# Layer 1 of a two-layer decoder as one list of small steps in TensorE's order

## The chip, the cores and the metric

The kernel runs on one core of a Trainium2 chip. The metric is the device time of one execution in microseconds, as the median of three runs.

## The reference

The input x has 256 tokens of 1024 features. Layer 0 is stick-breaking attention and a squared-ReLU MLP; layer 1 is native sparse attention (NSA) and the same kind of MLP; a final norm ends it. The change touches layer 1's attention and the keys and values that it shares:

```python
kv = (hn @ w_kv).reshape(b, s, 3, 2, NSA_KV_GROUPS, HEAD_DIM)   # hn = rms_norm(h, kv_norm)
hid = jax.nn.gelu(jnp.einsum('bncgf,cfe->bncge', blk, cmp_w1))   # blk: windows of 32 tokens of kv[:, :, 0]
cmp = jnp.einsum('bncge,ced->bncgd', hid, cmp_w2)                # compressed keys and values
...
q = proj[..., :NSA_HEADS * DH]; gates = sigmoid(proj[..., NSA_HEADS * DH:] + gate_b)
q_rot = partial_rope(q)
p_cmp = softmax(q . k_cmp);  o_cmp = p_cmp . v_cmp               # masked
p_sel = softmax(q_rot . k_sel); p_w = softmax(q_rot . k_w)       # causal; selected blocks and window
o = gates[0] * o_cmp + gates[1] * o_sel + gates[2] * o_win
h = h + o @ w_o
```

There are 16 heads of 64 in 4 key groups. With 256 tokens all 4 blocks are selected and the window reaches all tokens, so both of these branches are dense causal attention.

## The kernel before

Every large product is computed in three matmuls: a float32 weight is split into a rounded part wh (a CAST on ACT, L96) and the rest wl (a subtract on DVE, L97), the activations likewise, and `mm3` (L146) issues the three products at L147, L148 and L149. Weights come as a stream of 1 MB loads. `feed` appends a load to the stream when the program is set up, and the stream is loaded and split in that order. `fetch` issues a load on SP into one of three raw buffers, when the second half of an earlier one has been split. `W(i)` forces load i to be split, in two halves; `step()` splits one half more if fewer than three loads lie ahead of the present one. The split tiles wh and wl are rings of three.

PSUM has eight banks in two rings of four: `bank` gives one of the first ("a"), `bank2` of the second ("z"). An engine that writes a bank waits until the readers of its last contents are done. A scheduler orders the instructions of ACT, DVE and POOL by their dependencies; PE keeps the program's order where `strict[0]` is set (L142).

Layer 1's attention is the function `nsa`. Its pieces, with the short names that this text gives them (a digit is the index of a load's first and second half, of a head pair or of a group):

- kv (`kv_proj`): a key/value projection, 8 blocks of `mm3` per half; ACT scales it out of PSUM (L534 and after).
- gt, `gather`, gp: transposes for the compressed windows, their assembly on DVE, ACT and POOL, and the gates.
- rt: a table for the rotation. kt (`keys_tr`): transposed keys. `keys_rope`: rotation of the keys on POOL.
- cw (`cw_proj`): the hidden layer of the compression, accumulated in one bank ph.
- q00, q01, ..., q31 (`q_proj`): half 0 or 1 of the query projection of group 0 to 3. After half 1 ACT copies the bank out (qu, L680), and the rotation follows: a shuffle on DVE (L683), a multiply on POOL (L684), a multiply and an add on DVE (L685, L686: qr).
- gelu (L697 to L707, ACT and DVE), ch (`cmp_kv`: transposes of the hidden layer, bank pht), ck (`cmp_kv2`: compressed keys kcb by DVE at L727, values vcb at L734, banks pkc and pvc).
- cp (`cmp_probs`): scores against the compressed keys (bank psc) and their softmax; ct (`cmp_tr`): its transposes (bank pct), copied by ACT to pcT.
- S0 to S7 (`scores`): eight score matmuls of a pair of heads into four banks z; eight reductions on DVE (L799: nm), eight exponentials on ACT (L801); then a reciprocal and a product with the gates on DVE (L803, L805: rs), and four multiplies on POOL (L810), which scale the probabilities pe. The scaling is called M0 to M7 here.
- T0 to T7 (`turn`): twelve transposes of pe into three banks ptp, copied to pT by ACT, DVE (the middle one, L825) and ACT.
- V0 to V7 (`values`): probabilities times values in a bank po; ACT and DVE take oT out of it (L230, L231).
- o000 and so on (`o_proj`: half of the rows, half of the columns, block): the output projection with oT, into four accumulators acc. Then the residual adds, and xn, the transposes for the MLP.

The order is written out by hand. PE does, after the first half of the second kv:

```
rt gt0 kv11 gt1 gp kv20 cw00 kv21 cw01 kt0 q00 kt1 q01 cw10 q10 cw11 S0 q11 S1 q20 q21 ch T0 S2 ck
q30 cp0 T1 S3 q31 ct0 V0 T2 S4 o000 V1 T3 cp1 S5 o001 V2 T4 ct1 S6 o002 V3 T5 S7 o003 V4 T6
o010 o011 V5 o012 T7 o013 V6 V7 o100 o101 o102 o103 (residual) o110 o111 xn o112 o113
```

Of the kernel before, what the change touches and what calls it, by code (L numbers as in the profile page):

```python
# [39 lines left out]
def hybrid_kernel(ctx, tc, x, xcols, eye, gcols, gfin, wqk, wv, wo0, wkv, wq, wg, rot, wo1, w1, w2, cw1, cw2, cpos, gate_b, consts, out):  # L40
# [85 lines left out]
    i_kv = [[feed(wkv[n, i], 2048) for i in range(2)] for n in range(2)]  # L126
    i_kv.append([feed(wkv[2, 0], 2048)])
    i_c = [[feed(cw1[0, 0], 2048)]]
    i_kv[2].append(feed(wkv[2, 1], 2048))
    i_c[0].append(feed(cw1[0, 1], 2048))  # L130
    i_q = [feed(wq[0], 2048)]
    i_c.append([feed(cw1[1, 0], 2048)])
    i_q.append(feed(wq[1], 2048))
    i_c[1].append(feed(cw1[1, 1], 2048))
    i_q += [feed(wq[g], 2048) for g in range(2, NG)]
    i_o1 = [[feed(wo1[n, i], 2048) for n in range(2)] for i in range(2)]
# [351 lines left out]
    def nsa(xk, pt0, ap):  # L488
# [145 lines left out]
        kv_proj(0, 0)  # L634
        kv_proj(0, 1)
        strict[0] = True
        xq = xt_tiles("q")
        for half in range(2):
            xt_evac(pts[half], half, 2, xq)
        kv_proj(1, 0)  # L640

        pr = bank2("pr")
        for t in range(T):
            mm(pr[:, t * P:(t + 1) * P], rstd[t].to_broadcast([P, P]), ident, t == 0, True)
        for a in range(2):
            nc.vector.scalar_tensor_tensor(cs[:, a, :], pr[:, 0:T * P], -1.0, cs[:, a, :], op0=OP.mult, op1=OP.mult)
        gather_tr(0)
        kv_proj(1, 1)
        gather_tr(1)
        gather(0)  # L650
        gate_proj()
        gather(1)
        keys_rope(0)
        ph = bank2("ph")
        kv_proj(2, 0)
        cw_proj(0, 0)
        kv_proj(2, 1)
        keys_rope(1)
        cw_proj(0, 1)
        kT = big([P, NG, 2, T * P], F32, "kT")  # L660
        keys_tr(0)
# [27 lines left out]
        q_proj(0, 0)
        keys_tr(1)  # L690
        qu = big([P, NG, 2, T * P], F32, "qu")
        qr = big([P, NG, 2, T * P], F32, "qr")
        q_proj(0, 1)
        cw_proj(1, 0)
        q_proj(1, 0)
        cw_proj(1, 1)
        hx = sp.tile([M, 512], F32, name="hx", tag="y")  # L697
        nc.scalar.copy(hx, ph[DH:DH + M, :])
        nc.vector.tensor_add(hx, ph[0:M, :], hx)
        hu = sp.tile([M, 512], F32, name="hu", tag="y")  # L700
        nc.scalar.activation(hu, hx, AF.Square, scale=0.044715 ** 0.5)
        nc.vector.scalar_tensor_tensor(hu, hu, 1.0, hx, op0=OP.add, op1=OP.mult)
        nc.vector.tensor_scalar(hu, hu, -25.0, None, op0=OP.max)
        nc.scalar.activation(hu, hu, AF.Exp, scale=-GELU_C)
        nc.scalar.activation(hu, hu, AF.Ln, bias=1.0)
        nc.scalar.activation(hu, hu, AF.Exp, scale=-1.0)
        nc.vector.tensor_mul(hu, hu, hx)  # L707

        def cmp_kv():
# [330 lines left out]
```

## Time and profile before

| | us |
|---|---|
| median of three runs | 639.63 (639.62 to 640.43) |
| the profiled execution's own time | 641.18 |
| its span | 639.4 |
| PE busy | 622.3 (97%) |
| DVE busy | 430.2 (67%) |
| ACT busy | 355.2 (56%) |
| POOL busy | 59.7 (9%) |

The profile is of one execution; times in its rows count from the start of the span. Layer 1's attention with its keys and values lies between 300 and 454 us. A matmul's busy time overlaps the next one's, so the length of a step is best read from its first start to the next step's first start. The granted clock is a share of full speed.

### The profile page before, as it was taken

The page shows a single profiled execution, that of the slowest core. Times are in us where ns is not written, and L with a number is a line of the kernel's source. Part 1 is how long each engine was busy: PE and PEld are TensorE (multiplying, and loading weights), DVE is VectorE, ACT ScalarE, POOL GpSimd, SP SyncE. Part 2 cuts the span into 40 slices and gives each one's busy share as a digit, 9 for nine tenths or more (in the row PEclk, how much of TensorE's full clock was granted, in tenths as well). Part 3 has the DMA queues.
Part 4 walks back from the last instruction along what each step waited for, and adds up shares of the span by engine and source line. Part 5 has one row for each costly group of instructions (what it writes and reads, how often), then busy time and mean ns, then how long its engine had stood idle before and what let it go on. Part 6 is the DMA issues. An engine that isn't in the chain of part 4 may idle for free.

```text
span 639.4 us, 9091 instructions
## 1 busy us (share of the span) xinstructions
PE 622.3 (97%) x3561; PEld 521.9 (82%) x3561; DVE 430.2 (67%) x672; ACT 355.2 (56%) x604; POOL 59.7 (9%) x78
## 2 busy tenths in 40 slices
PE   9999999999999999999999988999999999999995
PEld 6798987888888888888889776667888888888884
DVE  5677887676665656657896996662776566656554
ACT  5766666564444444443947875772564444454433
POOL 0100000000000000001151266350000000000000
PEclk9999999999999999999999998899999999999998
DMA  8953333545555554544456521203346455655501
GB/s 271 411 203 133 132 132 132 191 144 202 189 198 197 198 198 173 207 157 153 166 206 249 210 102 67 100 1 133 131 169 207 161 199 186 202 194 197 198 0 67
DMA packets 18331, 108.12 MB, mean 169 GB/s; under 512 B 2416, under 2 KB 3312, under 8 KB 6384
## 3 DMA queue, kind: packets, MB, share of 16 engines
q1 hardware_dynamic: 16992, 105.84, 46.1%
q10 hardware_dynamic: 1296, 1.70, 0.8%
q8 instruction: 28, 0.46, 0.3%
q14 instruction: 15, 0.12, 0.1%
HBM read 106.48 MB, written 1.05 MB: 168 GB/s over the span
## 4 chain that ended last, share of the span: by engine, by line
PE 83%; DVE 8%; ACT 3%; issue 2%; DMA 2%; POOL 1%; SPq 0%; POOLq 0%; ACTq 0%; DVEq 0%
PE pu L152 27%; PE acc L147 11%; PE acc L149 11%; PE acc L148 11%; PE po L152 3%; DVE wl L97 3%; PE z L152 2%; PE pk L147 2%; PE pk L149 2%; PE pk L148 2%; PE qk L147 1%; PE ptp L155 1%; PE qk L148 1%; PE qk L149 1%; ACT wh L96 1%
## 5 line engine op out<-in xcount | busy, mean ns | idle before, releaser
L97 DVE TENSOR_TENSOR wl<-raw,wh 128x1024 fp32r<-128x1024 f32 (+1 forms) x200 | 238.4, 1227 | 119.5 <-ACT wh L96 119.1
L96 ACT CAST wh<-raw 128x1024 fp32r<-128x1024 f32 (+1 forms) x200 | 197.6, 1033 | 100.0 <-PE acc L149 45.8
L152 PE MATMUL pu<-xn,wh 128*128 128x512 f32 x512 | 130.1, 392 | 0.6 <-DVE xn L222 0.6
L152 PEld LDWEIGHTS pu<-xn,wh 128*128 128x128 f32 x512 | 93.8, 188 | 19.6 <-DVE xn L222 1.8
L147 PE MATMUL acc<-wh,hh 128*128 128x512 f32 x256 | 100.2, 391 | 0.0
L148 PE MATMUL acc<-wl,hh 128*128 128x512 f32 x256 | 100.1, 391 | 0.0
L149 PE MATMUL acc<-wh,hl 128*128 128x512 f32 x256 | 99.6, 390 | 0.0
L152 PEld LDWEIGHTS pu<-xn,wl 128*128 128x128 f32 x512 | 70.9, 190 | 5.0
L152 PE MATMUL pu<-xn,wl 128*128 128x256 f32 x512 | 73.9, 282 | 0.0
L149 PEld LDWEIGHTS acc<-wh,hl 128*128 128x128 f32 x256 | 48.1, 188 | 10.7 <-DVE hl L311 0.4
L147 PEld LDWEIGHTS acc<-wh,hh 128*128 128x128 f32 x256 | 48.2, 188 | 9.7 <-ACT hh L310 0.6
L310 ACT CAST hh<-ms 128x512 fp32r<-128x512 f32 x32 | 19.8, 620 | 64.9 <-DVE ms L306 64.9
L148 PEld LDWEIGHTS acc<-wl,hh 128*128 128x128 f32 x256 | 48.2, 188 | 8.8
L304 ACT COPY mr<-pu 128x256 f32<-128x256 f32 x64 | 23.6, 369 | 29.2 <-PE pu L152 29.2
L147 PE MATMUL qk<-xa,wh 128*128 128x256 f32 x128 | 37.0, 289 | 0.0
L148 PE MATMUL qk<-xa,wh 128*128 128x256 f32 x128 | 36.2, 283 | 0.0
L149 PE MATMUL qk<-xa,wl 128*128 128x256 f32 x128 | 36.2, 283 | 0.0
L311 DVE TENSOR_TENSOR hl<-ms,hh 128x512 fp32r<-128x512 f32 x32 | 22.1, 691 | 19.9 <-ACT hh L310 19.9
L801 ACT ACTIVATE pe<-pe,nm 128x256 f32<-128x256 f32 (+1 forms) x64 | 28.3, 443 | 11.1 <-DVE nm L799 11.1
L810 POOL TENSOR_TENSOR pe<-pe,rs 128x512 f32<-128x512 f32 (+1 forms) x32 | 31.7, 1019 | 27.6 <-ACT oT L230 11.8
L305 DVE TENSOR_TENSOR mu<-pu,mr 128x256 f32<-128x256 f32 x64 | 26.7, 417 | 5.8 <-ACT mr L304 5.8
L149 PE MATMUL acc<-wh,oT 128*128 128x512 f32 x64 | 25.5, 398 | 2.3 <-DVE oT L231 2.3
(177 smaller groups left out, 881.9 us busy)
## 6 DMA issues: line engine op xcount, KB each, us to landing
raw<-in_w SPq DMA_DIRECT2D x64, 1024.0 KB, 4.8
raw<-in_wo SPq DMA_DIRECT2D x8, 1024.0 KB, 4.8
raw<-in_wqk SPq DMA_DIRECT2D x7, 1024.0 KB, 4.9
raw<-in_wkv SPq DMA_DIRECT2D x6, 1024.0 KB, 4.8
raw<-in_cw SPq DMA_DIRECT2D x4, 1024.0 KB, 5.2
raw<-in_wq SPq DMA_DIRECT2D x4, 1024.0 KB, 4.8
raw<-in_wv SPq DMA_DIRECT2D x8, 256.0 KB, 4.1
raw<-in_wv SPq DMA_DIRECT2D x4, 512.0 KB, 8.0
```

What stands on the lines that cost most here:

```text
L96: nc.scalar.copy(h[:, r], raws[j][:, r])
L97: nc.vector.tensor_sub(lo[:, r], raws[j][:, r], f32(h[:, r]))
L147: pe(nc.tensor.matmul(o, a[0], b[0], start=first, stop=False, skip_group_check=True))
L148: pe(nc.tensor.matmul(o, a[0], b[1], start=False, stop=False, skip_group_check=True))
L149: pe(nc.tensor.matmul(o, a[1], b[0], start=False, stop=last, skip_group_check=True))
L152: pe(nc.tensor.matmul(o, a, b, start=first, stop=last, skip_group_check=True))
L304: nc.scalar.copy(r[:, q], pu[f][:, 256:512])
L305: nc.vector.tensor_add(u[:, q], pu[f][:, 0:256], r[:, q])
L310: nc.scalar.copy(hh, sv)
L311: nc.vector.tensor_sub(hl, sv, f32(hh))
L801: nc.scalar.activation(e, e, AF.Exp, scale=-1.0, bias=nm[:, hd, t, b:b + 1], accum_out=rs[:, hd, t, b:b + 1])
L810: nc.gpsimd.tensor_tensor(sv, sv, rs[:, hd, t, :][:, :, None].to_broadcast([P, 2, n]), op=OP.mult)
```

## The change

A table `NSA` at the head of the file lists 104 steps of layer 1's attention, and a loop calls a function for each. The functions are those of before, cut smaller: the rotation (`q_rot`, "qr") is taken out of `q_proj`, the scaling (`weights`, "M") out of `scores`, and the gelu, the residual adds and xn are steps of their own. A turn, a score or a value step names the ring of each of its banks by a letter. The loads are fed in the order in which the list names their first use: kv20, kv21, c00, q0, c01 where it was kv20, c00, kv21, c01, q0. Six steps "w" call `step()` once more. The bank ph is of ring "a" now. PE keeps the list's order through the whole stage, where it was free to move the last part before.

```diff
+NSA = (
...
+    ('cw', 1, 1), ('q', 1, 1), ('S', 0, 'zzaz'), ('M', 0), ('ge',), ('qr', 1), ('S', 1), ('M', 1), ('q', 2, 0),
+    ('q', 2, 1), ('ch',), ('w',), ('T', 0, 'zaa'), ('S', 2, 'azaz'), ('ck',), ('q', 3, 0), ('T', 1), ('qr', 2),
...
+)
...
+    for f, *a in NSA:
+        if f == "kv":
+            i_kv[a[0]][a[1]] = feed(wkv[a[0], a[1]], 2048)
+        elif f == "cw":
+            i_c[a[0]][a[1]] = feed(cw1[a[0], a[1]], 2048)
+        elif f == "q" and a[1] == 0:
+            i_q[a[0]] = feed(wq[a[0]], 2048)
...
+        def q_rot(g, eng="p"):
...
+            nc.vector.stream_shuffle(qx, qu[:, g], swap)
+            (nc.gpsimd if eng == "p" else nc.vector).tensor_tensor(
+                qr[:, g], qu[:, g], cs[:, 0:1, :].to_broadcast([P, 2, T * P]), op=OP.mult)
...
-        def scores(p):
+        pools = {"a": bank, "z": bank2}
+
+        def scores(p, bks="zzzz"):
             g, j = divmod(p, 2)
-            z1 = [bank2(f"z1{hd}").rearrange("p (b k) -> p b k", b=2) for hd in range(2)]
+            z1 = [pools[bks[hd]](f"z1{hd}").rearrange("p (b k) -> p b k", b=2) for hd in range(2)]
...
+            live["s", p] = rs, pes
+
+        def weights(p):
+
+            rs, pes = live.pop(("s", p))
             nc.vector.reciprocal(rs, rs)
...
+        strict[0] = True
+        do = {"kv": kv_proj, "xq": tokens_q, "rt": rot_tables, "gt": gather_tr, "ga": gather, "gp": gate_proj, "kr": keys_rope,
+              "cw": cw_proj, "kt": keys_tr, "q": q_proj, "qr": q_rot, "ge": gelu, "ch": cmp_hid, "ck": cmp_kv, "S": scores,
+              "M": weights, "T": turn, "V": values, "cp": cmp_probs, "ct": cmp_tr, "o": o_proj, "r": residual, "xn": tokens_n,
+              "w": step}
+        for f, *a in NSA:
+            do[f](*a)
         strict[0] = False
```

Every engine has as many instructions as before. PE's order is now:

```
kv11 gt1 gp gt0 kv20 kv21 cw00 q00 cw01 rt kt0 q01 cw10 kt1 q10 cw11 q11 S0 S1 q20 q21 ch T0 S2 ck
q30 T1 cp0 S3 q31 ct0 V0 S4 V1 T2 cp1 T3 o000 S5 V2 ct1 T4 o001 S6 V3 V4 S7 T5 o002 o003 T6
o010 o011 V5 T7 o012 o013 o100 V6 V7 o101 o102 o103 (residual) o110 xn o111 o112 o113
```

Three places of the engines' order in detail. First PE at S0 and S1, before; ph is the end of cw11, z10 to z01 are the four banks of a pair's scores, pq is the half q11:

```order
L152 MATMUL ph_2967<-wh_3207,blk_2954 128x256
L152 MATMUL ph_2967<-wl_3208,blk_2954 64x256
L152 MATMUL z10_3283<-kT_3092,qr_3147 128x512
L152 MATMUL z11_3284<-kT_3092,qr_3147 128x512
L152 MATMUL z00_3285<-kT_3092,qr_3147 128x256
L152 MATMUL z01_3286<-kT_3092,qr_3147 128x256
L147 MATMUL pq_3206<-xq_2784,wh_3182 128x256
...
L149 MATMUL pq_3206<-xq_2784,wl_3183 128x256
L152 MATMUL z10_3351<-kT_3092,qr_3147 128x512
L152 MATMUL z11_3352<-kT_3092,qr_3147 128x512
L152 MATMUL z00_3353<-kT_3092,qr_3147 128x256
L152 MATMUL z01_3354<-kT_3092,qr_3147 128x256
```
And now:

```order
L166 MATMUL ph_3034<-wh_3187,blk_3094 128x256
L166 MATMUL ph_3034<-wl_3188,blk_3094 64x256
L161 MATMUL pq_3223<-xq_2678,wh_3149 128x256
...
L163 MATMUL pq_3223<-xq_2678,wl_3150 128x256
L166 MATMUL z10_3305<-kT_3136,qr_2677 128x512
L166 MATMUL z11_3306<-kT_3136,qr_2677 128x512
L166 MATMUL z00_3307<-kT_3136,qr_2677 128x256
L166 MATMUL z01_3308<-kT_3136,qr_2677 128x256
L166 MATMUL z10_3355<-kT_3136,qr_2677 128x512
L166 MATMUL z11_3356<-kT_3136,qr_2677 128x512
L166 MATMUL z00_3357<-kT_3136,qr_2677 128x256
L166 MATMUL z01_3358<-kT_3136,qr_2677 128x256
```
The half q11 stood between the two pairs of scores and now stands ahead of both; z00 of S0 is of the other ring.

Then PE at cp0 and T1, before; pq is the end of q30, psc is cp0, ptp are the three banks of T1, z10 is S3:

```order
L149 MATMUL pq_3528<-xq_2784,wl_3318 128x256
L152 MATMUL psc_3557<-kcb_3274,qu_3146 128x30 x8
L152 LDWEIGHTS cbf_76
L152 MATMUL psc_3557<-cmb_78,cbf_76 128x120
L152 LDWEIGHTS cbf_76
L152 MATMUL psc_3557<-cmb_78,cbf_76 128x120
L155 MATMUL ptp_3580<-ident_70,pe_3361 128x128 x4
L155 MATMUL ptp_3586<-ident_70,pe_3361 128x128 x2
L155 MATMUL ptp_3586<-ident_70,pe_3362 128x128 x2
L155 MATMUL ptp_3592<-ident_70,pe_3362 128x128 x4
L152 MATMUL z10_3598<-kT_3092,qr_3147 128x512
```
And now:

```order
L163 MATMUL pq_3521<-xq_2678,wl_3265 128x256
L169 MATMUL ptp_3551<-ident_70,pe_3365 128x128 x4
L169 MATMUL ptp_3557<-ident_70,pe_3365 128x128 x2
L169 MATMUL ptp_3557<-ident_70,pe_3366 128x128 x2
L169 MATMUL ptp_3563<-ident_70,pe_3366 128x128 x4
L166 MATMUL psc_3578<-kcb_2679,qu_2676 128x30 x8
L166 LDWEIGHTS cbf_76
L166 MATMUL psc_3578<-cmb_78,cbf_76 128x120
L166 LDWEIGHTS cbf_76
L166 MATMUL psc_3578<-cmb_78,cbf_76 128x120
L166 MATMUL z10_3606<-kT_3136,qr_2677 128x512
```
T1 and cp0 have changed places.

Then DVE behind the scaling factors of S3 (rs of L805), before; qx and qr are the rotation of q3, wl a half of a weight, oT of L231 what PE needs for o000, pT of L825 the middle of T2:

```order
L805 TENSOR_TENSOR rs_3607<-rs_3607,gates_2675 128x8
L683 STREAM_SHUFFLE qx_3661<-qu_3146 128x512
L685 TENSOR_TENSOR qx_3661<-qx_3661,cs_2664 128x512
L97 TENSOR_TENSOR wl_3918<-raw_3388,wh_3917 128x1024
L686 TENSOR_TENSOR qr_3147<-qr_3147,qx_3661 128x512
L231 TENSOR_TENSOR oT_3672<-po1_3673,oT_3672 128x256
L825 COPY pT_3686<-ptp_3693 128x512
L799 ISA pe_3715,nm_3713<-z10_3705,nmask_3280 128x256
```
And now, where pe and z10 are S4, the first oT is V0's and the second V1's:

```order
L822 TENSOR_TENSOR rs_3615<-rs_3615,gates_2675 128x8
L682 STREAM_SHUFFLE qx_3713<-qu_2676 128x512
L685 TENSOR_TENSOR qx_3713<-qx_3713,cs_2664 128x512
L112 TENSOR_TENSOR wl_3792<-raw_3278,wh_3791 128x1024
L811 ISA pe_3695,nm_3693<-z10_3685,nmask_2685 128x256
L811 ISA nm_3693 128x1
L245 TENSOR_TENSOR oT_3671<-po1_3672,oT_3671 128x256
L811 ISA pe_3695,nm_3693<-z10_3685,nmask_2685 128x256
...
L811 ISA pe_3696,nm_3693<-z01_3688,nmask_2685 128x128
...
L686 TENSOR_TENSOR qr_2677<-qr_2677,qx_3713 128x512
L112 TENSOR_TENSOR wl_3792<-raw_3278,wh_3791 128x1024
L245 TENSOR_TENSOR oT_3671<-po1_3718,oT_3671 128x256
```
The subtract for V0's oT stood behind the add of qr and now stands ahead of it, among the reductions of S4, which came after T2 before.

## Rows read from the trace of the kernel before

**Rows 1.** The page's first part: busy time, share of the span and instructions of each engine.
```profile
PE 622.3 (97%) x3561; PEld 521.9 (82%) x3561; DVE 430.2 (67%) x672; ACT 355.2 (56%) x604; POOL 59.7 (9%) x78
```

**Rows 2.** PE's waits, 250 to 460 us: instruction, what it waited for, us in total, times, longest.
```profile
PE acc L149 <- DVE oT L231: 2.3, 1, 2.3
PE ptp L155 <- ACT qu L680: 1.7, 1, 1.7
PE psc L152 <- DVE kcb L727: 1.2, 1, 1.2
PE acc L147 <- ACT oT L230: 1.0, 1, 1.0
PE z L152 <- DVE nm L799: 0.5, 1, 0.5
PE z L152 <- DVE qr L686: 0.5, 1, 0.5
```

**Rows 3.** Windows of 20 us: busy us of each engine, granted clock, DMA share, GB/s.
```profile
350.00:370.00 20.00, 19.01 (x145) 16.70 (x144) 18.33 (x44) 16.82 (x38) 5.70 (x5) 1.00 0.62 229
370.00:390.00 20.00, 17.06 (x126) 14.14 (x125) 17.93 (x59) 12.61 (x41) 12.45 (x12) 0.91 0.30 105
390.00:410.00 20.00, 17.73 (x123) 12.28 (x122) 13.43 (x48) 12.68 (x42) 9.01 (x9) 0.91 0.19 68
```

**Rows 4.** Timeline of PE, 380 to 389: start, us, instruction, idle before and releaser.
```profile
380.55 0.28 PE L149 MATMUL pq<-xq,wl 128*128 128x256 f32 x1
381.99 2.13 PE L152 MATMUL psc<-kcb,qu 128*128 128x30 f32 x16 [1.16 <-DVE kcb L727]
...
384.12 2.77 PE L155 MATMUL ptp<-ident,pe 128*128 128x128 f32 x12
```

**Rows 5.** Timeline of PE, 356 to 366: S0, the half q11, S1.
```profile
357.51 1.53 PE L152 MATMUL z<-kT,qr 64*128 64x512 f32 x6 [0.46 <-DVE qr L686]
359.57 0.67 PE L152 MATMUL z<-kT,qr 64*128 64x256 f32 x2 [0.53 <-DVE nm L799]
360.16 0.39 PE L147 MATMUL pq<-xq,wh 128*128 128x256 f32 x1
...
363.22 1.56 PE L152 MATMUL z<-kT,qr 64*128 64x512 f32 x8
```

**Rows 6.** Timeline of PE, 396 to 426: V1, T3, the second output block, V4.
```profile
401.24 2.83 PE L152 MATMUL po<-pT,vs 128*64 128x256 f32 x16
...
404.60 1.53 PE L155 MATMUL ptp<-ident,pe 128*128 128x128 f32 x12
...
409.58 0.50 PE L147 MATMUL acc<-wh,oT 128*128 128x512 f32 x1
...
424.73 1.52 PE L152 MATMUL po<-pT,vs 128*64 128x256 f32 x16
```

**Rows 7.** Timeline of POOL, 360 to 440: the scalings M0, M3, M4, M7.
```profile
367.44 4.08 POOL L810 TENSOR_TENSOR pe<-pe,rs 128x512 f32<-128x512 f32 x4
...
392.92 4.61 POOL L810 TENSOR_TENSOR pe<-pe,rs 128x512 f32<-128x512 f32 x4 [4.92 <-ACT qu L680]
...
405.08 3.18 POOL L810 TENSOR_TENSOR pe<-pe,rs 128x512 f32<-128x512 f32 x4 [6.32 <-ACT oT L230]
...
427.68 5.23 POOL L810 TENSOR_TENSOR pe<-pe,rs 128x512 f32<-128x512 f32 x4 [3.56 <-DVE rs L805]
```

**Rows 8.** The instructions of tile rs, 355 to 430: min/median/max ns of one.
```profile
L805 DVE TENSOR_TENSOR rs<-rs,gates x8: 154/173/1323, 366.0 to 427.3; 128x8 f32<-128x8 f32 x8
```

**Rows 9.** Timeline of DVE, 390 to 402: rotation of q3, then oT0.
```profile
398.79 0.69 DVE L686 TENSOR_TENSOR qr<-qr,qx 128x512 f32<-128x512 f32 x1 [2.30 <-POOL qr L684]
399.39 0.42 DVE L231 TENSOR_TENSOR oT<-po,oT 128x256 fp32r<-128x256 f32 x1
```

**Rows 10.** The page's DMA issues: count, KB each, us to landing.
```profile
raw<-in_cw SPq DMA_DIRECT2D x4, 1024.0 KB, 5.2
```

**Rows 11.** Timeline of PE, 452 to 456: the first matmul of the last MLP.
```profile
454.53 0.39 PE L152 MATMUL pu<-xn,wh 128*128 128x512 f32 x1
```

More of the change, by code (lines that the diff above doesn't have):

```diff
@@ L124, in hybrid_kernel @@
     i_m = [feed_mlp(0)]
[L126 to L136, printed above, removed]
+    i_kv, i_c, i_q, i_o1 = [{} for _ in range(3)], [{}, {}], {}, [{}, {}]
+    for f, *a in NSA:
[5 more added lines that the diff above has]
+            i_q[a[0]] = feed(wq[a[0]], 2048)
+        elif f == "o" and a[1] not in i_o1[a[0]]:
+            i_o1[a[0]][a[1]] = feed(wo1[a[1], a[0]], 2048)
     i_m.append(feed_mlp(1))
@@ L553, in nsa @@
         blk = [None, None]
+        ph = None
         def gather_tr(c):
@@ L586, in gather @@
             blk[c] = [b[:, j] for b in bs for j in range(n)]
+        kT = None
         def keys_rope(br):
@@ L599, in cw_proj @@
         def cw_proj(c, i):
+            nonlocal ph
+            if c == 0 and i == 0:
+                ph = bank("ph")
             w = W(i_c[c][i])
@@ L633, in nsa @@
         live = {}
[L634 to L661, printed above, removed]
+        qu = big([P, NG, 2, T * P], F32, "qu")
+        qr = big([P, NG, 2, T * P], F32, "qr")
         def q_proj(g, half, hooks={}):
@@ L689, in nsa @@
[L689 to L709, printed above, removed]
+        def q_rot(g, eng="p"):
+            qx = ap.tile([P, 2, T * P], F32, name="qx", bufs=2)
+            nc.vector.stream_shuffle(qx, qu[:, g], swap)
+            (nc.gpsimd if eng == "p" else nc.vector).tensor_tensor(
+                qr[:, g], qu[:, g], cs[:, 0:1, :].to_broadcast([P, 2, T * P]), op=OP.mult)
+            nc.vector.tensor_tensor(qx, qx, cs[:, 1:2, :].to_broadcast([P, 2, T * P]), op=OP.mult)
+            nc.vector.tensor_add(qr[:, g], qr[:, g], qx)
@@ new lines, in nsa, with tokens_q, rot_tables @@
+        swap = [*range(8, 16), *range(8), *range(16, 32)]
+        xq = xt_tiles("q")
+        def tokens_q(half):
+            xt_evac(pts[half], half, 2, xq)
+        def rot_tables():
+            pr = bank2("pr")
+            for t in range(T):
+                mm(pr[:, t * P:(t + 1) * P], rstd[t].to_broadcast([P, P]), ident, t == 0, True)
+            for a in range(2):
+                nc.vector.scalar_tensor_tensor(cs[:, a, :], pr[:, 0:T * P], -1.0, cs[:, a, :], op0=OP.mult, op1=OP.mult)
@@ new lines, in gelu @@
+        def gelu():
+            hx = sp.tile([M, 512], F32, name="hx", tag="y")
+            nc.scalar.copy(hx, ph[DH:DH + M, :])
+            nc.vector.tensor_add(hx, ph[0:M, :], hx)
+            hu = sp.tile([M, 512], F32, name="hu", tag="y")
+            nc.scalar.activation(hu, hx, AF.Square, scale=0.044715 ** 0.5)
+            nc.vector.scalar_tensor_tensor(hu, hu, 1.0, hx, op0=OP.add, op1=OP.mult)
+            nc.vector.tensor_scalar(hu, hu, -25.0, None, op0=OP.max)
+            nc.scalar.activation(hu, hu, AF.Exp, scale=-GELU_C)
+            nc.scalar.activation(hu, hu, AF.Ln, bias=1.0)
+            nc.scalar.activation(hu, hu, AF.Exp, scale=-1.0)
+            nc.vector.tensor_mul(hu, hu, hx)
+            live["h"] = hu
@@ L811, in scores, with turn @@
             live["e", p] = pes
-        def turn(p, bks=(bank, bank, bank)):
+        def turn(p, bks="aaa"):
             pes = live.pop(("e", p))
@@ L817, in turn @@
             for i in range(3):
-                pt = bks[i]("ptp")
+                pt = pools[bks[i]]("ptp")
                 for m in range(4):
@@ L828, in turn, with values @@
             live["t", p] = pT
-        def values(p, bk=bank):
+        oT = None
+        def values(p, bk="a"):
+            nonlocal oT
             g = p // 2
-            po = bk("po1")
+            if p == 0:
+                oT = pair([NP, T * P], "oT")
+                oT = oT[:, 0], oT[:, 1]
+            po = pools[bk]("po1")
             pT = live.pop(("t", p))
```

77 lines of the change are left out of this document (20 added, 57 removed), and 10 rows, old and new, of the table NSA.

## Prediction

> **What bounds the kernel now.** I read the page's first part, then TensorE's waits, then the windows, then the timelines of PE, DVE and POOL in the stretch that the change reorders. The page [rows 1] shows PE busy for 97% of the span, so the kernel is one long PE queue, and a reordering without new work can only win what PE now loses. The waits of PE between 250 and 460 us [rows 2] show where it waits in layer 1: 2.3 us for a DVE subtract that makes the attention output oT, 1.7 for the ACT copy of a query tile qu, 1.2 for kcb, 1.0 for another oT, twice 0.5 at the first scores. That is 7.2 us in six stops. The windows [rows 3] show a second loss: in 370–390 and in 390–410 the mean granted clock is 0.91 instead of 1.00, which is a stretch at 1.2 GHz in each.
>
> **What of this can be won.** (a) The six stops, 7.2 us. (b) Each stop costs a little more than its idle time: matmuls of q30 follow each other by 0.12 us, the last one starts at 380.55, cp0 at 381.99, so 1.32 us are lost where 1.16 are called idle [rows 4]. Six such differences of 0.15 make 0.9. (c) The first scores S0 run from 357.51 to 360.16, 2.65 us; S1, the same eight matmuls, take 1.56 [rows 5]. Of the 1.1 between them 0.53 stands in (a), 0.6 is new. (d) The slow clock: turn T1 takes 2.77 us where T3 takes 1.53 [rows 4, 6], the sixteen matmuls of V1 on vs take 2.83 where those of V4 take 1.52 [rows 6]; 1.24 + 1.31, and some 0.4 in the neighbours. Together 2.95. All in all 7.2 + 0.9 + 0.6 + 2.95 = 11.7 us (rounded). More than this the change cannot give: every engine has the same instructions, only their order, their banks and so their waits differ.
>
> **The change part by part.**
>
> *Half of q1 ahead of S0.* S0 waits for the rotated queries (0.46) and then for banks of scores that DVE has not yet reduced (0.53) [rows 5]. With q11 ahead, PE reaches S0 some 3 us later (q11 runs from 360.16 to 363.22), at 359.9 if nothing else stops it, while the rotation of q0 hangs on q01, which both orders have three steps and more ahead of S0; by my addition of ACT's and DVE's lists it is ready at 355.7. Both losses go: 0.46 + 0.15 + 1.1 = 1.7. What comes: S1 now follows S0 directly, and three of its four banks are those of S0. DVE reduces a 256-wide half in about 0.35 and a 128-wide one in about 0.21, so the third and fourth bank come free some 0.6 after PE wants them. I take 0.6; the ends are 0 and 1.1, what S0 paid for the same dependence [rows 5].
>
> *ch and T0.* T0's third bank was the one in which q2 had been projected, and it stopped 1.7 for ACT's copy qu2 out of it, behind S1's exponentials and a cast [rows 2]. The new letters give T0 other banks, so this goes (1.85). T0 then needs the scaling M0, which takes POOL 4.1 us [rows 7]. Its factors are ready after the eight reductions of S0, two gelu steps and the rotation of q1, by my addition of DVE's list at 366.3, so M0 ends at 370.3; PE is at T0 at 369.7, and needs three of the four multiplies. I take 0.2, ends 0 and 0.7.
>
> *S2.* The bank of q2 now goes to its first scores, right behind T0, so that the same copy is waited for one turn (1.4 us) later, still behind the exponentials of S1. I take 0.6 (ready by my addition at 371.9); ends 0 and 1.7, its price for T0 before [rows 2].
>
> *ck.* Its bank is the middle one of T0, freed by DVE's copy, and ahead of that copy on DVE stands a tiny product rs·gates. It takes 0.17 us in the median of eight, but 1.32 at most [rows 8], and here it meets the rotation of q2 on POOL. I take 1.1 with what is behind it; ends 0 and 1.3.
>
> *T1 ahead of cp0.* cp0 waited 1.2 for kcb, the DVE copy of ck's result [rows 2, 4]. T1 now lies between them, 1.5 us of work, and q30 before it. The wait goes with its extra (1.3), and T1 does not lose by coming earlier: M1 on POOL ends 0.8 before T1 by my addition.
>
> *S4 and V1 between V0 and the first output o000.* At 398.79 DVE adds the rotation of q3, after 2.30 us of waiting for POOL, whose multiply for it stands behind the scaling M3, which ends at 397.5; the subtract that makes oT0 stands right behind that add on DVE, and PE's o000 waits for it [rows 2, 7, 9]. Now oT0's subtract comes ahead of the add, and o000 comes after V1, T2, cp1 and T3: some 7 us later. The 2.3 goes, with its 0.15. New: V0 needs pcT, an ACT copy, right after ct0, 0.2 (ends 0 and 0.5).
>
> *T6 to o010.* The 1.0 us for oT there [rows 2] goes, since o002, o003 and T6 separate V4 from o010.
>
> *Scaling apart from the scores, on POOL.* From M1 on each scaling is done 0.8 to 10 us ahead of its turn, at 4.6 us each [rows 7]. Nothing; rival D is the case that it is not.
>
> *Loads in list order, splits a half further ahead.* The loads of cw land 5.2 us after issue in the median [rows 10]; SP issues the same ten of this stage, each when a ring buffer is free, with kv21 and c00, and q0 and c01, changed over. The tightest is the second half of cw0: its two halves are split by 343.3 by my addition, wanted at 343.35. Taken as nothing; ends 0 and 1.1.
>
> *The end.* S7's last bank waits for a subtract of oT (0.2), and the transposes for the MLP now stand before o111 and wait for the residual (0.3); ends 0 and 0.5 each. The three matmuls of o100 that stood among o011 return to their place, at no cost.
>
> **The sum.** New waits: 0.6 + 0.2 + 0.6 + 1.1 + 0.2 + 0.2 + 0.3 = 3.2 us. None of them is longer than 1.1, and the two stops that came just ahead of the slow clock were 1.2 and 2.3 [rows 2]; so I let the slow clock go too. Gain 11.7 − 3.2 = 8.5. The first matmul of the last MLP, now at 454.53 [rows 11], should come at about 446. The profiled execution took 641.18 us, which gives 632.7; the median of three runs, 639.63, lies 1.55 below that execution, so the forecast is **631.1 us**. A measurement of this kernel can tell about 0.2%, some 1.3 us, from no change.
>
> **Rivals.** *B, DVE becomes the bound between 360 and 390.* DVE is busy 18.3 and 17.9 us of 20 in 350–370 and 370–390 [rows 3], and the gain squeezes its work into fewer microseconds. For it: the long forms of rs·gates, and M7, 5.23 us beside weight splits where 3.18 is the price with DVE quiet [rows 7, 8]. Against it: in 370–390 DVE also idles, since it waits for PE itself. Then the new waits come to their upper ends in this stretch, 1.1 + 0.7 + 1.7 + 1.3, with 0.5 each for the three behind: 6.3 in place of 3.2, and 634.2 us. Chance 0.2. By the Trainium skill (SBUF — State Buffer, Who interferes with whom) a DVE instruction with two inputs in SBUF and a GpSimd instruction that reads SBUF exclude one another for a whole instruction; the rows of rs·gates and of M7 agree. Applied to every such pair of my addition, rather than to the pairs seen long before, it would add 0.6, which is 631.7.
>
> *C, the slow clock comes back.* From ct0 to o000 PE will have ct0, V0, S4, V1, T2, cp1 and T3, some 11 us in which no projection runs, and small stops before them. Against it: in the old order T3, cp1 and S5 follow each other from 404.60 to 409.58, and T3 is fast [rows 6]. A slow stretch costs 1.24 to 1.31 and some 0.2 beside it, 1.5; two of them make 634.1. Chance 0.14 for two or more; one (632.6) is inside the forecast's own range. The Trainium skill (TensorE: Matmul & The Clock Gate, Part 4: PE-mode transpose) says that transposes on PE do not count as busy for the clock gate, which speaks against a list that puts T2, cp1 and T3 one behind the other. The fast T3 row does not bear it out. By the rule the slow clock would fall in that place, and the time would be 632.6 to 634.1.
>
> *D, slower than before: the scaling chain on POOL.* M0 to M7 and two rotations now stand in one queue from 366.3, and T7, which wants M7, comes at about 424.5 by my layout. With 4 us for the rotations and a copy, eight scalings may take (58.2 − 4) / 8 = 6.8 us each before T7 is late at all, and 8.0 each make it 9.8 late, so that the kernel is over 0.2% slower, at 641. The rows have 3.18 to 5.23 [rows 7]. Chance 0.03.
>
> *E, no gain:* new waits that eat all, 11.7 of them, nearly twice the ends of B; 639.6. Chance 0.03. That the order does not take effect is excluded by the lists of the engines, which show it.
>
> **How the numbers follow.** Forecast case 0.6 at 631.1, with its own range from 628 (every loss gone gives 641.18 − 11.7 − 1.55 = 627.9) to 633; B 0.2 at 634.2, C 0.14 at 634.1, D 0.03, E 0.03. The range from 628.0 to 635.2 takes in A, most of B and of C. Faster by over 0.2%: 0.94; within: 0.03; slower: 0.03.
>
> **What would show it.** Right: PE's waits in this stage have no stop over 1.2 us; oT's subtract and kcb are gone from the list, and z behind the reductions, z behind ACT's copy qu and pkc behind a DVE copy are in it, 3 us with the small ones; the granted clock is 1.00 in every window of the stage; the last MLP begins near 446. Wrong in the way of B: stops of over 1.5 us at S1, S2 and ck with DVE over 18.5 in 20. Wrong in the way of C: T or V rows of 2.7 us. Wrong in the way of D: ptp behind POOL's multiply in the list.

## The result and the profile after

The changed kernel takes 632.86 us (median of four runs, 631.96 to 633.67), the kernel before 640.03 beside it (639.62 to 642.14). The ratio is 0.9872 with a 95% interval of 0.9855 to 0.9889: 1.3% faster. The forecast was 631.1 with a range of 628.0 to 635.2.

The first part of the page of the changed kernel (busy time of each engine) beside [rows 1]:

```profile
PE 619.8 (98%) x3561; PEld 521.7 (83%) x3561; DVE 428.3 (68%) x672; ACT 354.5 (56%) x604; POOL 57.6 (9%) x78
```
PE has as many instructions as before. PE's waits from 250 to 460 us (what it waited for, us in total, times, longest), beside [rows 2]:

```profile
PE pkc L166 <- DVE pT L842: 0.6, 1, 0.6
PE pq L161 <- DVE nm L811: 0.5, 1, 0.5
PE po L166 <- ACT pcT L780: 0.3, 1, 0.3
...
PE z L166 <- DVE nm L811: 0.2, 1, 0.2
PE z L166 <- ACT qu L677: 0.2, 1, 0.2
```
The six stops of before, 7.2 us, are all gone. The five that stand here are 1.8 us, none over 0.6; one kind, z behind the reductions, was there before too, with 0.5 at S0 where it is now 0.2 at S1. The windows of 20 us (busy time of PE, weight loads, DVE, ACT, POOL, then granted clock, DMA share and GB/s), beside [rows 3]:

```profile
310.00:330.00 20.00, 20.00 (x109) 17.50 (x109) 15.73 (x20) 14.73 (x24) 3.30 (x5) 0.94 0.56 217
...
350.00:370.00 20.00, 19.82 (x150) 17.60 (x150) 18.89 (x46) 16.53 (x36) 4.82 (x4) 1.00 0.72 270
370.00:390.00 20.00, 18.70 (x155) 16.07 (x155) 19.36 (x67) 15.73 (x56) 11.24 (x13) 1.00 0.30 107
390.00:410.00 20.00, 19.68 (x153) 13.84 (x150) 16.91 (x57) 15.63 (x52) 10.39 (x11) 1.00 0.23 81
```
The two places with the clock at 0.91 are gone too. A new one stands in 310 to 330, where the kernel before had 1.00. PE's timeline shows it (start, us, instruction); pk is kv11 and then kv20, ptc are gt1 and gt0, pg is gp:

```profile
322.98 1.03 PE L169 MATMUL ptc<-ident,kd 128*128 128x128 f32 x8
323.77 3.73 PE L166 MATMUL pg<-wgp,xq 128*128 128x96 f32 x32
327.35 1.93 PE L169 MATMUL ptc<-ident,kd 128*128 128x128 f32 x8
328.93 0.77 PE L161 MATMUL pk<-wh,xk 128*128 128x512 f32 x1
```
PE waits for nothing here. gt1 lasts 0.79 us from its start to the next, gt0 1.58, and the first four matmuls of kv20 1.85 (to 330.78) where four take 0.91 at full speed. The slow clock costs 0.79 + 0.94 = 1.7 us. Last the first matmul of the last MLP, beside [rows 11]:

```profile
446.70 0.39 PE L166 MATMUL pu<-xn,wh 128*128 128x512 f32 x1
```
From the first matmul of the stage (299.70 before, 300.31 after) to this one the stage took 154.83 us and now takes 146.39. The stage gains 8.4 us. The profiled executions differ by 7.9 (641.18 and 633.31), since the one of the changed kernel reached the stage 0.6 later, in a part of the program that is the same; the medians of four differ by 7.2.

### The profile page after: what moved, and what is told of

The parts are those of the page before. It is cut to its first block, busy times and chain, and to the rows that moved or that the text cites. A ratio compares the mean times of both kernels' runs of the same rounds, so it can differ in the third digit from the quotient of the medians.

```text
span 631.5 us, 9096 instructions
## 1 busy us (share of the span) xinstructions
PE 619.8 (98%) x3561; PEld 521.7 (83%) x3561; DVE 428.3 (68%) x672; ACT 354.5 (56%) x604; POOL 57.6 (9%) x78
## 4 chain that ended last, share of the span: by engine, by line
PE 83%; DVE 7%; ACT 4%; DMA 3%; issue 2%; SPq 0%; POOLq 0%; POOL 0%; ACTq 0%; DVEq 0%
PE pu L166 27%; PE acc L161 11%; PE acc L162 11%; PE acc L163 11%; PE po L166 3%; DVE wl L112 3%; DMA raw<-in_wv 2%; PE pk L161 2%; PE pk L162 2%; PE pk L163 2%; PE z L166 2%; DMA raw<-in_wqk 2%; PE qk L161 1%; PE qk L162 1%; PE qk L163 1%
## 5 line engine op out<-in xcount | busy, mean ns | idle before, releaser
L827 POOL TENSOR_TENSOR pe<-pe,rs 128x512 f32<-128x512 f32 (+1 forms) x32 | 30.1, 970 | 25.5 <-DVE rs L822 16.1
```

The lines of the kernel that those rows point to most:

```text
L827: nc.gpsimd.tensor_tensor(sv, sv, rs[:, hd, t, :][:, :, None].to_broadcast([P, 2, n]), op=OP.mult)
```

## The experiments

In all of them the comparison is with the changed kernel's 632.86 us and with its trace; every ratio in brackets is to the kernel before, with its 95% interval. The kernel before, measured again beside each group, has medians of 639.76 to 640.81, so a difference of under 1 us between two of these kernels is not clear by the times alone. "Stage" is the time from the stage's first matmul to the last MLP's first.

### What the places of the rotation and of the scaling are worth

PE's order stays that of the changed kernel in three kernels; only the place in the list at which the scaling (M) and the rotation (qr) are issued goes back. M0 and M1 stand right behind their scores in the changed kernel already, so what goes back of the scaling is M2 to M7. First both; the diff shows the first of the moves:

```diff
-('q', 1, 1), ('S', 0, 'zzaz'), ('M', 0), ('ge',), ('qr', 1), ('S', 1), ('M', 1), ('q', 2, 0), ('q', 2, 1), ('ch',), ...
+('q', 1, 1), ('qr', 1), ('S', 0, 'zzaz'), ('M', 0), ('ge',), ('S', 1), ('M', 1), ('q', 2, 0), ('q', 2, 1), ('qr', 2), ('ch',), ...
```

> The steps of PE stay as in the changed kernel; the scaling M is written right behind its scores and the rotation right behind its projection again. The prediction costed this separation at nothing. Theory now, from the run with the old stretch behind ct0: the rotation of q3 then stands ahead of S4's reductions on DVE and waits 2.3 us for POOL's M3, so PE waits 1.5 to 3.5 us around V1 and T2 and the clock may fall there: 634.5 to 638. Rival (the prediction's nothing): 632.9 within 0.6.

Measured: 641.81 us (1.0029, 1.0014 to 1.0044), slower than the kernel before. All of the gain is gone, more than the theory expected. To part the two, only the scaling behind its scores:

> Only the scaling M is written right behind its scores again; the rotation stays where the changed kernel has it. Of the stops that the run with both joined showed, the 2.2 us of ck's values behind POOL's copy hv (which stood behind M1) should be this one's. Theory: that stop and its cover, and perhaps one slow clock, 2.4 to 4: 635.3 to 637. Rival: nothing by itself, since POOL's order hangs on the rotation; 632.9 within 0.8.

Measured: 631.63 us (0.9857, 0.9828 to 0.9885), and the same waits as the changed kernel, to 0.1 us. The rival holds in the waits, though the time is 1.2 below the changed kernel's, where it allowed 0.8; the two intervals overlap. So no loss is seen from the scaling's place, and the 2.2 us behind hv that I gave to it belong to the rotation, as the next kernel shows. And only the rotation behind its projection:

> Only the rotation is written right behind its projection again; the scaling stays. Theory: DVE's add for q1 stands ahead of S0's reductions and waits for POOL, so S1's banks come free late (1.6 us), and the add for q3 stands ahead of S4's reductions and waits 2.3 us for POOL behind M3, so T2 stops 2.6 us and the clock falls once or twice (1.3 to 3): 638 to 640. Rival: without M1 in its way POOL is early enough, and the time is 632.9 to 634.

Measured: 641.33 us (1.0008, 0.9992 to 1.0024), even with the kernel before, and over the theory's end. The stage runs from 300.77 to 455.76, 154.99 us, 8.6 more than the changed kernel's, with PE's steps in the same order. PE's waits in it:

```profile
PE pvc L167 <- POOL hv L726: 2.2, 1, 2.2
PE ptp L170 <- DVE nm L812: 1.8, 1, 1.8
PE z L167 <- DVE nm L812: 1.6, 2, 0.9
```
The first kind of stop, z behind the reductions, is S1 waiting for the banks of S0. DVE's timeline in the same kernel shows why (qx and qr are the rotation of q1, pe<-z a reduction of S0):

```profile
363.59 0.42 DVE L812 CUSTOM_DVE_ANT_0 pe<-z,nmask 128x256 f32<-128x256 f32 x1
...
364.28 0.73 DVE L683 STREAM_SHUFFLE qx<-qu 128x512 f32<-128x512 f32 x1
...
365.24 0.74 DVE L686 TENSOR_TENSOR qx<-qx,cs 128x512 f32<-128x512 f32 x1
...
366.25 0.68 DVE L687 TENSOR_TENSOR qr<-qr,qx 128x512 f32<-128x512 f32 x1
...
367.48 0.28 DVE L812 CUSTOM_DVE_ANT_0 pe<-z,nmask 128x128 f32<-128x128 f32 x1
```
The shuffle, the multiply and the add for q1 stand among the eight reductions of S0, which take from 363.59 to 367.76. In the changed kernel the rotation of q1 comes behind them, and they run without a break, first and last:

```profile
363.17 0.41 DVE L811 CUSTOM_DVE_ANT_0 pe<-z,nmask 128x256 f32<-128x256 f32 x1
...
365.18 0.28 DVE L811 CUSTOM_DVE_ANT_0 pe<-z,nmask 128x128 f32<-128x128 f32 x1
```
That is 2.3 us for the eight in place of 4.2. The add for q1 does not wait for POOL here, as the theory had it; the rotation's own time among the reductions is enough. The later scaling then crowds POOL (pe<-pe,rs are M0 and M1, hv is a copy that ck needs):

```profile
369.80 5.75 POOL L828 TENSOR_TENSOR pe<-pe,rs 128x512 f32<-128x512 f32 x4 [4.37 <-DVE rs L823]
375.72 4.17 POOL L828 TENSOR_TENSOR pe<-pe,rs 128x512 f32<-128x512 f32 x4 [0.17 <-DVE rs L823]
379.85 1.26 POOL L684 TENSOR_TENSOR qr<-qu,cs 128x512 f32<-128x512 f32 x1
381.05 1.05 POOL L726 COPY hv<-hidT 128x480 f32<-128x480 f32 x1
```
M0 starts at 369.80 and takes 5.75, M1 follows at once, and the rotation of q2 and hv stand behind both: pvc of ck waits 2.2 us for hv. The third stop, 1.8 at T2, is a bank that a reduction of S4 frees late, again behind q3's rotation. On the fall of the clock: the windows 370–390 and 390–410 have 0.86 and 0.91 in this run.

### The stretch behind ct0

```diff
-('V', 0), ('S', 4), ('qr', 3), ('V', 1), ('T', 2, 'aza'), ('cp', 1), ('T', 3, 'azz'), ('o', 0, 0, 0), ('M', 4),
+('qr', 3), ('V', 0), ('T', 2, 'aza'), ('S', 4), ('o', 0, 0, 0), ('V', 1), ('T', 3, 'azz'), ('cp', 1), ('M', 4),
```

> The stretch behind ct0 in its old order: rotation of q3, V0, T2, S4, o000, V1, T3, cp1. On DVE the subtract of the first oT then stands behind the add of q3's rotation again. Theory: o000 waits 2.0 to 2.5 us for oT, and a stretch of slow clock may follow (1.3 to 1.5): 635 to 637. Rival: the wait of before came of POOL's later M3 and is gone with the earlier scalings; then o000 waits under 0.5 and the time is 632.9 to 633.4.

Measured: 637.97 us (0.9963, 0.9945 to 0.9981), 5.1 more than the changed kernel. DVE's queue has the picture of [rows 9] again, with the same 2.30 us:

```profile
396.37 0.69 DVE L686 TENSOR_TENSOR qr<-qr,qx 128x512 f32<-128x512 f32 x1 [2.30 <-POOL qr L683]
396.97 0.42 DVE L245 TENSOR_TENSOR oT<-po,oT 128x256 fp32r<-128x256 f32 x1
397.31 0.68 DVE L842 COPY pT<-ptp 128x512 f32<-128x512 f32 x1
```
The add waits for POOL, the subtract of oT stands behind it, and behind that the copy out of a bank of T2. PE stops at S4 for that bank, ahead of o000, and o000 then runs at the slow clock (0.79 us for its first matmul, 0.50 in [rows 6]):

```profile
398.04 0.82 PE L166 MATMUL z<-kT,qr 64*128 64x256 f32 x2 [3.56 <-DVE pT L842]
398.79 0.79 PE L161 MATMUL acc<-wh,oT 128*128 128x512 f32 x1
```
The same stop as before, one step earlier in PE's queue. Next, o000 as near to V0 as it was, but with the subtract ahead of the add on DVE:

```diff
-('qr', 3), ('V', 1), ('T', 2, 'aza'), ('cp', 1), ('T', 3, 'azz'), ('o', 0, 0, 0), ('M', 4),
+('qr', 3), ('o', 0, 0, 0), ('V', 1), ('T', 2, 'aza'), ('cp', 1), ('T', 3, 'azz'), ('M', 4),
```

> The order of the changed kernel, but o000 right behind S4, ahead of V1: as near to its oT as it was before, while the subtract on DVE stays ahead of q3's add. Theory: it is the place of the subtract in DVE's queue that counts, so o000 waits under 0.5 us and the time is 632.9 to 633.4. Rival: the distance of 7 us between V0 and o000 counts; then it waits 1.5 to 2.5 and the time is 634.5 to 636.

Measured: 633.52 us (0.9889, 0.9855 to 0.9922). o000 waits 1.0 us, between the two expectations, and the clock does not fall there:

```profile
394.53 0.50 PE L163 MATMUL acc<-wh,oT 128*128 128x512 f32 x1 [1.02 <-DVE oT L245]
```
So with the subtract ahead of the add 1.0 us of the 2.3 is left when o000 comes at once, and the distance in PE's queue takes care of that. In the changed kernel the same DVE rows read:

```profile
395.08 0.41 DVE L245 TENSOR_TENSOR oT<-po,oT 128x256 fp32r<-128x256 f32 x1
...
397.29 0.68 DVE L686 TENSOR_TENSOR qr<-qr,qx 128x512 f32<-128x512 f32 x1
```
The subtract (395.08) runs 2.2 us before the add (397.29), and the add no longer waits: by the time DVE has reduced S4, POOL's multiply is done (at 397.1).

### cp0 and T1, S0 and q11

cp0 right behind q30, ahead of T1:

```diff
-('q', 3, 0), ('T', 1), ('qr', 2), ('w',), ('cp', 0), ('M', 2),
+('q', 3, 0), ('cp', 0), ('T', 1), ('qr', 2), ('w',), ('M', 2),
```

> Only the order of cp0 and T1 goes back: cp0 right behind q30. Theory of the prediction: T1 between them was what took away the wait for kcb, so psc waits again, 1.2 to 1.3 us, and the time is 634.1. Rival, from the trace of the changed kernel: DVE's copies of kcb end at about 380.4 and q30 only at 381.5, so the wait is gone without the swap; no wait, 632.9 within 0.2.

Measured: 632.52 us (0.9873, 0.9836 to 0.991), and psc is not among PE's waits. The rival holds for the wait; the time is no longer than the changed kernel's. The trace of the changed kernel has the reason. DVE's copy of kcb, and PE at the end of q30, where T1 starts:

```profile
379.92 0.44 DVE L737 COPY kcb<-pkc 64x60 f32<-64x60 f32 x2
```
```profile
381.56 1.47 PE L169 MATMUL ptp<-ident,pe 128*128 128x128 f32 x12
```
kcb is done more than a microsecond before cp0 could start in either order. Before, where psc waited [rows 2], the copy started 5.5 us behind ck's first matmul (375.92), and now 3.5 (376.38). Ahead of it on DVE stood the add of q2's rotation, which now comes after it, at 382.86. DVE before:

```profile
378.42 1.18 DVE L686 TENSOR_TENSOR qr<-qr,qx 128x512 f32<-128x512 f32 x1
...
381.40 0.44 DVE L727 COPY kcb<-pkc 64x60 f32<-64x60 f32 x2
```
So by these rows DVE's order took that wait away; no run puts this add alone back.

S0 ahead of q11:

```diff
-('cw', 1, 1), ('q', 1, 1), ('S', 0, 'zzaz'), ('M', 0), ('ge',), ('qr', 1), ('S', 1), ('M', 1),
+('cw', 1, 1), ('S', 0, 'zzaz'), ('M', 0), ('ge',), ('q', 1, 1), ('qr', 1), ('S', 1), ('M', 1),
```

> Only S0 goes back ahead of the half q11; S1 stays behind it. Theory of the prediction: q11 ahead of S0 is worth 1.7 (rotation and late reductions) less 0.6 to 1.2 that S1 behind S0 pays, so the time is 0.5 to 1.1 more than the changed kernel's 632.9: 633.4 to 634.0, with S0 waiting for qr and its last banks. Rival, from the trace of the changed kernel: q0's rotation is done at 359.2, when cw11 ends, and all four banks of S0 are free; S0 then waits for nothing, S1 finds its banks free, and the time is 0.5 to 1.2 less: 631.7 to 632.4.

Measured: 633.05 us (0.988, 0.9859 to 0.9902), neither gain nor loss. PE's timeline (z are S0 and S1, pht is ch):

```profile
357.21 1.56 PE L166 MATMUL z<-kT,qr 64*128 64x512 f32 x8 [0.20 <-DVE qr L686]
...
361.76 1.56 PE L166 MATMUL z<-kT,qr 64*128 64x512 f32 x8
...
372.05 0.46 PE L721 MATMUL pht<-ident,hu 60*128 60x60 f32 x4 [2.78 <-DVE hu L714]
```
Both scores run in 1.56 us, as the rival said, where the two together take 4.2 in the changed kernel:

```profile
361.99 3.44 PE L166 MATMUL z<-kT,qr 64*128 64x512 f32 x14
365.61 0.67 PE L166 MATMUL z<-kT,qr 64*128 64x256 f32 x2 [0.18 <-DVE nm L811]
```
But ch then waits 2.8 for the last product of the gelu, and the window 370–390 has the clock at 0.91. The stage takes 146.74 us, with full speed behind gp; the changed kernel's without its fall there would be 144.7. So q11 ahead of S0 buys nothing at the scores; it buys time for the gelu. The gelu ahead of S0, on top of two small edits that come below:

> The kernel of e9_small_waits with the gelu ahead of S0 and S0 ahead of the half q11. Theory: S0 and S1 then find their banks free (the 1.1 and 0.2 us of pq and z behind the reductions go), and ch does not wait for the gelu's last product, which made up for that gain when only S0 was moved (2.8 us): 1.2 less than e9_small_waits, 629.3. Rival: the wait for the gelu or for the scaling M0 stays at 1 us or more and takes the gain: 630.5 to 631.5.

Measured: 633.73 us (0.9892, 0.9868 to 0.9915), 3.2 more than its base. The rival holds, and past its end: the gelu's wait goes, T0 waits for POOL instead and runs at the slow clock. PE at T0, and POOL (M0 and M1 run together, eight multiplies):

```profile
372.54 2.60 PE L169 MATMUL ptp<-ident,pe 128*128 128x128 f32 x12 [1.93 <-POOL pe L827]
```
```profile
368.00 9.17 POOL L827 TENSOR_TENSOR pe<-pe,rs 128x512 f32<-128x512 f32 x8
```
Three tries in this place move one wait between S1's banks, ch and T0: DVE is busy 18.9 and 19.4 us of 20 in 350–370 and 370–390 of the changed kernel.

### Loads and extra splits

The loads fed in the old order (kv20, c00, kv21, c01, q0) and the extra splits "w" left out (the table has 99 steps, five of them "w", and not the 104 and six that stand ahead of the prediction):

> The changed kernel with the loads fed in their old order and without the six extra split steps. Theory (the prediction costed both at nothing): 632.9 within 0.8, and no wait for wh or wl of cw or q in PE's list. Rival: a weight half comes late where PE now arrives earlier, a stop of 1 to 2.4 us (one or two splits) at cw01, q10 or q20, and 634 to 635.3.

Measured: 633.93 us (0.9887, 0.9856 to 0.9918), 1.1 more than the changed kernel, with the interval wide beside that; it lies between the two expectations. The trace speaks more plainly: q00, which the rival did not name, stops twice, for the wh and the wl of its weight, and the clock in 340–350 is 0.83:

```profile
341.10 0.39 PE L163 MATMUL pq<-xq,wh 128*128 128x256 f32 x1 [0.47 <-ACT wh L111]
...
342.63 0.38 PE L165 MATMUL pq<-xq,wl 128*128 128x256 f32 x1 [1.02 <-DVE wl L112]
```
The stage takes 148.36 us (299.73 to 448.09), 2.0 more than the changed kernel's, and 3.7 more than the 144.7 that it would be without the fall of the clock behind gp, which this profile does not have. This execution is the longest of its four. So the two together are worth 1.1 us by the medians and up to 3.7 in this profile; which of them, the order of the loads or the extra splits, was not parted.

### The clock at the gate projection, and the small waits

gt0 back to its old place:

```diff
-('kv', 1, 0), ('kv', 1, 1), ('gt', 1), ('gp',), ('gt', 0),
+('kv', 1, 0), ('gt', 0), ('kv', 1, 1), ('gt', 1), ('gp',),
```

> Only the first transposes gt0 go back to their old place between kv10 and kv11; all else is the changed kernel. Theory: the slow clock of the changed kernel (gt0 takes 1.93 us instead of 1.03, from about 327 to 331) comes of gt1, gp and gt0 standing one behind the other without a projection, 5.9 us from 322.98 to 328.93. Then the granted clock is 1.00 from 318 to 345, gt0 takes 1.03, and the time is 1.7 us less than the changed kernel's 632.9: about 631.2. Rival: the clock fell for what the other engines and the transfers did there (DMA share 1.02 in 323 to 326). Then it falls in the same place, and the time stays at 632.9.

Measured: 632.24 us (0.987, 0.9833 to 0.9908). The clock falls all the same, right behind gp (pg):

```profile
324.25 3.73 PE L166 MATMUL pg<-wgp,xq 128*128 128x96 f32 x32
327.82 0.57 PE L161 MATMUL pk<-wh,xk 128*128 128x512 f32 x1
...
331.78 0.39 PE L162 MATMUL pk<-wl,xk 128*128 128x512 f32 x1
```
kv20's matmuls come 0.43 us apart from 328.2 to 331 and 0.23 later. Its runs part as those of the changed kernel do: 631.3 and 631.5 us at a mean clock of 0.998 and 0.997, 633.0 and 633.8 at 0.995. So gt0's place does not decide it. Nor do the transfers that the rival named: from 323 to 326 the DMA share is 0.51 in this profile, where the clock fell, and 1.01 in that of the kernel with S0 ahead of q11, where it did not. The next kernel has the same program up to T0, and its profile has 1.00 there:

```diff
 (gt0 back as above)
-('T', 0, 'zaa')
+('T', 0, 'aza')
-('V', 0), ('S', 4), ('qr', 3), ('V', 1)
+('S', 4), ('qr', 3), ('V', 0), ('V', 1)
```

> The changed kernel with gt0 in its old place and two edits against its waits: the banks of T0 are aza instead of zaa (ck's first bank is then freed by an ACT copy, not by the DVE copy behind rs·gates), and S4 stands ahead of V0 (so that ct0's copy is hidden). Theory: the waits pkc behind pT (0.6) and po behind pcT (0.3) leave the list, no new one over 0.3 comes, and the time is 0.9 less than with gt0 alone moved: 631.3. Rival: the wait moves on to the next bank or to the reductions of S4, and the time stays at 632.2.

Measured: 630.54 us (0.9846, 0.9824 to 0.9868), with the next one the fastest of all, 2.3 less than the changed kernel, though the two intervals overlap. Its stage takes 144.14 us (299.24 to 443.38), 2.25 less, of which 1.7 are the clock behind gp; so some 0.5 of the 0.9 us forecast for the two edits came. Of PE's waits the two aimed at are gone, and one of the others has doubled:

```profile
PE pq L161 <- DVE nm L811: 1.1, 1, 1.1
```
pq behind the reductions was 0.5. Then the gate projection in two halves, one on each side of kv20:

```diff
-        def gate_proj():
-            pg = bank("pg")
-            for k in range(NK):
+        def gate_proj(half):
+            if half == 0:
+                live["pg"] = bank("pg")
+            pg = live["pg"]
+            for k in range(4 * half, 4 * half + 4):
...
-('kv', 1, 0), ('gt', 0), ('kv', 1, 1), ('gt', 1), ('gp',), ('ga', 0), ('kv', 2, 0),
+('kv', 1, 0), ('gt', 0), ('kv', 1, 1), ('gt', 1), ('gp', 0), ('ga', 0), ('kv', 2, 0), ('gp', 1),
```

> The kernel of e9_small_waits with the gate projection gp (3.7 us of small matmuls of 96 columns) cut in two halves, one ahead of kv20 and one behind it. Theory: the slow clock near 327 comes, in some executions, of the stretch without a projection around gp (4.4 to 5.9 us); halved, it is 2.6 and 1.8 us, and no execution falls to the slow clock there: mean clock 0.998 or more in every run and 630.5, with less spread between runs. Rival: the clock falls for another reason (transfers, other engines); then about half of the runs still show 0.994 to 0.995 and the time is that of e9_small_waits.

Measured: 630.64 us (0.9842, 0.982 to 0.9863), with a mean clock of 0.997 to 0.999 in all four runs and a spread of 0.8 us. Its base had 0.998 in four runs (629.98 to 630.78) and 0.995 in one (632.46). This is close to what the theory says (0.998 or more), but four runs against one exception in five don't show it. The two medians are the same.

Over the profiles of the changed kernel and of the twelve experiments, the clock fell behind gp in five (mean 0.89 from 320 to 335) and not in eight (1.00), also between kernels whose program is the same up to there. So this fall belongs to the execution more than to the order. In the four runs of the changed kernel the mean clock was 0.994 at 633.31 and 633.67 us, and 0.997 at 631.96 and 632.41.

## Why the prediction was right, and where it was not

The time was forecast as 631.1 and came out as 632.86, at the upper end of the main case's own range (628 to 633). The main case happened. The gain was forecast as 8.5 us, and the stage gained 8.4 in the profiled executions, but that closeness is luck: the new waits cost about 1.6 us (the 11.7 less the 10.1 that the stage would have gained at full speed) in place of 3.2, and a fall of the clock that was not forecast took 1.7 back. The 1.8 us by which the time is longer come from outside the stage's sum. The profiled execution reached the stage 0.6 later than the one before, and the median of the changed kernel lies 0.45 below its profiled execution, where the forecast took off the 1.55 of the kernel before. Point by point:

**What can be won, 11.7 us: right.** The six stops and the two slow stretches went, all of them.

**New waits, 3.2 us: right in kind, too large.** They are 1.8 us of idle time. z behind the reductions and pq behind them, 0.7 together, but S0 and S1 take 4.2 us where two would take 3.0 without waits, 1.2 in place of the 0.6 that I took. pkc behind DVE's copy 0.6 for 1.1, z behind qu2 0.2 for 0.6, po behind pcT 0.3 for 0.2. T0, S7 and the transposes xn don't wait. ck was priced by the long form of rs·gates; in the changed kernel the longest of the eight took 0.50 us, where [rows 8] has 1.32.

**"I let the slow clock go too": half right.** In the two old places, yes. A third place, behind gp, cost 1.7 us; no part of the prediction looked at it, because the kernel before has full speed there in its profile. Without it the profiled stage would have been 144.7.

**"Scaling apart from the scores, on POOL … Nothing": right for the scaling, and the later place of the rotation was given no price of its own.** That is the step that failed, though the sum did not suffer from it, since I added up the queues as they stand after the change. With the rotation alone back behind its projection the stage takes 155.0 us, as long as before, while PE's order is the new one. The gain that the prediction gave to the order of PE's steps hangs on the place of `q_rot` in the order of DVE and POOL. How much PE's order would win or lose by itself stays open: no run has the old order of PE with the later rotation, and none puts back T0's banks (1.85 us in the forecast) or the way from V4 to o010 (1.0).

**"T1 ahead of cp0 … the wait goes": the wait goes, not for this reason.** With cp0 first there is no wait either, since kcb is done 1.2 us earlier than q30.

**"Half of q1 ahead of S0 … Both losses go": not for this reason.** S0 ahead of q11 waits 0.2 us, not 1.7. The half q11 gives time to the gelu, whose last product ch would otherwise wait for, 2.8 us.

**S4 and V1 between V0 and o000: right.** With the old stretch DVE's add waits 2.30 us for POOL as in [rows 9], and the kernel loses 5.1 us, more than half of the gain: 3.56 of waiting and a slow clock behind it. With o000 near but the subtract ahead, 1.0 us of waiting.

**Loads, taken as nothing: right as a cost, but the change in them is needed.** In the changed kernel PE waits for no weight in this stage. The old order with fewer splits stops q00 for its weights (0.47 and 1.02). It feeds c01 ahead of q0, while PE now does q00 ahead of cw01; in my layout I looked at c01 as the tightest, not at q0.

**Rivals.** B did not come: DVE is busy 18.9 and 19.4 us of 20 there, more than the 18.5 named as its sign, but no stop is over 0.6. M7 took 5.15 us beside weight splits in the changed kernel, M5 and M6 3.18. The rule of the Trainium skill (SBUF — State Buffer, Who interferes with whom) agrees with that, but the 0.6 us more that I worked out from it did not come: no rs·gates took over 0.50. C did not come in its place, though one slow stretch came in another, behind gp, at 1.7 us where C has 1.5 for one. PE's timeline from T2 to o000:

```profile
395.74 1.53 PE L169 MATMUL ptp<-ident,pe 128*128 128x128 f32 x12
397.10 1.87 PE L166 MATMUL psc<-kcb,qu 128*128 128x30 f32 x16
...
398.93 1.48 PE L169 MATMUL ptp<-ident,pe 128*128 128x128 f32 x12
400.16 0.48 PE L161 MATMUL acc<-wh,oT 128*128 128x512 f32 x1
```
T2, cp1 and T3 follow one another at full speed, and the window 390–410 has 1.00. The Trainium skill (TensorE: Matmul & The Clock Gate, Part 4: PE-mode transpose) says that the full clock does not engage for transposes on PE; read as a rule for a stretch of turns, it would have the clock fall here, and the trace does not bear that out. Behind gp the turns of gt0 cannot be the reason alone, as with gt0 moved away it fell as well. D did not come: POOL's scaling is not among PE's waits. Nor did E: the gain is 7.2 us.

## What to carry to other kernels

Where a scheduler lays out the helper engines, moving a step in the program can move its instructions in their queues as well (the rotation here; the scaling's place made no difference); test which engine's order brings the gain by putting back the steps that the main engine does not run. A short chain that goes from one helper engine to another and back (here shuffle, multiply on POOL, add) held up everything behind it in DVE's queue, by 2.30 us in [rows 9]; issue such a chain late, behind what the main engine waits for. Where one wait is taken away and the time stays, look at the next wait in the same stretch before moving more: here, with DVE busy 19 of 20 us, the wait only changed its name in three tries.

## What was not expected of the hardware

The clock fell in places where PE did not wait at all: behind the gate projection's 96-column matmuls and the turns beside them, in five of thirteen profiles, with 1.7 us lost where it was worked out. Of kernels whose program is the same up to there, some fell in their profile and some did not, so one profile does not tell whether an order is free of it. What makes the difference between two executions stays open.
